# Ten of sixteen experts sorted by token count on the chip, the last four taken in one pass of four column tiles

## The chip, the cores and the metric

The kernel runs on one core of a Trainium2 chip. The metric is device time in microseconds (us); the median of three runs of the kernel before is 483.41 us (481.74 to 483.44). Traces come from the hardware profiler, one execution each. PE is TensorE's matmul, PEld its weight load, DVE is VectorE, ACT is ScalarE, POOL is GpSimd, SP is the engine whose queue issues nearly all DMAs.

## The reference, cut to what matters

A decoder block on 256 tokens (16 meta tokens in front make 272) with 1024 features: two mixers in parallel on a normalised input, then a mixture of 16 experts, then a norm. All of it is float32. The change concerns the experts alone.

```python
def hier_moe(u, wg_r, bg_r, we_r, be_r, w_gate, w_up, w_down):
    t = u.reshape(b * L, d)
    p_group = softmax(t @ wg_r + bg_r)             # 4 groups
    g_val, g_idx = top_k(p_group, 1)
    e_logits = (t @ we_r + be_r).reshape(-1, 4, 4)
    sel = take_along_axis(e_logits, g_idx[:, :, None], axis=1)[:, 0]
    top_v, top_i = top_k(sel, 2)                   # 2 of the group's 4 experts
    top_w = softmax(top_v)
    combine = ...                                  # (tokens, 16): 0 but for two experts
    for e in range(16):                            # w_gate[e], w_up[e]: 1024 x 512; w_down[e]: 512 x 1024
        h = silu(t @ w_gate[e]) * (t @ w_up[e])
        out = out + combine[:, e:e + 1] * (h @ w_down[e])
```

Each of the 256 tokens goes to two experts of one group, so an expert has 32 tokens in the mean. With the reference's inputs (seed 0) the experts 0 to 15 have 37, 31, 32, 36, 25, 24, 24, 27, 50, 39, 35, 38, 26, 32, 27 and 29 tokens; this was worked out from the reference and stands in no trace.

## The kernel before, in words

The program is written in order by hand, engine by engine; nothing reorders it. Up to about 235 us the trace shows the mixers: products with `w_in` and `w_out` in two float32r parts, the SSD and the short convolution between them. From 235 to 252 us stands the router: scores, for each expert the slot of each of its tokens (`ranks`, tile `rk`), and the largest token count (`most`, then the integer `mosti`, which every engine loads into a register).

The weights come as a stream of tiles of 1 MB (128 partitions x 8 KB), issued on SP's queue into a ring of slots in SBUF: `RING` slots that the whole program uses, `RING2` more for the experts. An expert matrix is 2 MB; a tile is a quarter of the rows of a matrix, of both experts of a pair (4 KB of each per partition). There are 96 tiles of experts, 12 to a pair: gate, up, down. When PE is done with a tile, `used(1)` gives its slot to the next tile of the stream; SP waits at that DMA until the slot is free, and everything behind it in SP's program waits too.

The experts go in 8 pairs (loop over `pair`, L1099). An expert has `CAP` = 64 slots; a pair fills the 128 columns of the array. Within a pair:

- `pick` makes a selection matrix P (tokens x 128 slots), `gather3` multiplies the normalised tokens by it and gives X, the tokens of both experts, transposed. The tokens stand in three bf16 parts (`hparts`), made by ACT and DVE in turn during the first pair.
- `half_product` (L965) multiplies X by the weights: for each of 8 slices k of the features, one matmul for each expert, 64 columns of the array each (`tile_position`), 512 wide; each shows as two records in the trace. Gate, then silu on ACT; up, then a product on DVE (`hb`).
- `back` and `turned` give the transposed selection, the weights of the tokens, and hb transposed; the down product is four slices of twice 512.
- `weighed` and `scatter` add the weighted rows to their tokens in four PSUM banks, within the next pair's gate product.

The first product of X for pair 0 is a plain float32 gather in the router; DVE scales it (`rows`, L1003). `weights` on DVE works out the combine weights and their three bf16 parts (`cparts`). After the last pair's up product stands `tc.If(rv > CAP)`: where an expert has more than 64 tokens, `over()` takes all pairs again from further slots; in the traced run it is not taken. The last pair's down product is in three pieces of 512, 256 and 256 columns, and the end of its stream in pieces too; then comes the last norm.

Of the kernel before, what the change touches and what calls it, by code (L numbers as in the profile page):

```python
# [20 lines left out]
RING, RING2 = 21, 3  # L21
# [14 lines left out]
def body(ctx, tc, x, meta_tokens, norm_mix, w_in, ssd_conv_w, ssd_conv_b, dt_bias, A_log, D_skip,  # L36
# [31 lines left out]
    between = []  # L68

    def load(n, pool=None):  # L70
        # the next n tiles of the stream
        for j in range(nload[0], min(nload[0] + n, NW + 96)):
# [28 lines left out]
            stream[j] = w  # L101

# [5 lines left out]
    rk = cp.tile([128, 2, NE], F32, name="rk")  # L108
    comb = cp.tile([128, 2, NE], F32, name="comb")
# [20 lines left out]
    # the meta tokens: partition 8 t + k has features 128 k to 128 k + 127 of token t  # L130
# [26 lines left out]
    # what is small goes between the large ones  # L157
# [29 lines left out]
    # the columns of one product are fewer than the array's  # L187
    f0 = slot("f0").bitcast(F32R)
    G.iota(sl, pattern=[[1, CAP]], base=-1024, channel_multiplier=0, allow_small_or_imprecise_dtypes=True)
# [54 lines left out]
    def x_part(b, n, c0=0, c1=512):  # L244
        # the residual goes to where the product with w_out will be added up
# [27 lines left out]
    def split_hi(i):  # L273
# [67 lines left out]
    def dt_softplus(n):  # L341
        # softplus(a) = max(a, 0) + log(1 + e), e = exp(-|a|); log(1 + e) = 2 atanh(e / (2 + e))
# [18 lines left out]
    def dt_sums():  # L361
        # sums of dA within tokens 0-127 and within tokens 128-271: for the keys ...
# [7 lines left out]
        # ... and for the queries  # L370
# [160 lines left out]
    def sums(key, t, n, kind):  # L531
# [7 lines left out]
        # in two parts that sum to it: one in the even rows, one in the odd ones  # L539
# [99 lines left out]
    # tiles of the ring that are not of the stream: the steps in which they are held  # L639
# [23 lines left out]
    def fill(i):  # L663
        # after step i: as many tiles of the stream as leave room for the others
# [110 lines left out]
    def logits(b, q):  # L775
        # the products of four parts of the features side by side
# [16 lines left out]
    def places(b, step):  # L793
        # how many of a set of four come before each (equal ones: the lower index first)
# [9 lines left out]
        else:  # L804
            # of the first two of their group, whose group is the first: 1 is more than no group
# [3 lines left out]
    def ranks(b):  # L809
        # slot of each token at each of its experts, less 1024; not negative where it isn't one of them  # L810
# [4 lines left out]
        V.scalar_tensor_tensor(rk[:, b], mem[:, b], -1024.0, p, op0=OP.mult, op1=OP.add)  # L815

    def pick(P, pair, b):
        V.tensor_tensor(P[:, b], sl[:, None].to_broadcast([128, 2, CAP]),
                        rk[:, b, 2 * pair:2 * pair + 2][:, :, None].to_broadcast([128, 2, CAP]), op=OP.is_equal)

    def gather(b, q, p, i0=0, i1=4):
        # one mark per bank: the first product in it clears the bank's marks of what has been written
        for i in range(i0, i1):
            T.matmul(p[:, i], hh[:, b].rearrange("p (m k) -> p k m", k=KT)[:, 4 * q + i],
                     P[:, b].rearrange("p s c -> p (s c)"), start=(b == 0 and i == 0), stop=(b == 1),
# [173 lines left out]
    def w_of(pair, kind, q):  # L999
        return stream[NW + 12 * pair + 4 * kind + q]  # L1000
# [234 lines left out]
```

## Time and profile before

| | us |
|---|---|
| median of 3 runs (lowest, highest) | 483.41 (481.74, 483.44) |
| the profiled execution: span from the first to the last instruction | 480.2 |
| PE busy in it | 456.1 |
| DVE, ACT, POOL busy | 234.7, 161.6, 64.8 |
| first product of pair 0, of pair 1, of pair 7 starts at | 252.19, 278.16, 441.98 |
| last down product ends at about | 470.5 |

Of the profiled execution only the span is given; the median of the runs is 3.2 us longer, which is what lies around the span. A busy PE is not PE at its peak: matmuls are pipelined and their ends are modelled, so a time between two starts of a repeated piece says more than a sum of busy times. A wait is read from the bracket behind a row of the timeline: how long the engine stood idle, and what ended it.

### The profile page before, as it was taken

How to read it: one execution, taken by the hardware profiler on the slowest of the kernel's cores; microseconds unless marked ns; L12 is line 12 of the kernel's file. 1: busy time of each engine (PE TensorE's matmuls, PEld its weight loads, DVE VectorE, ACT ScalarE, POOL GpSimd, SP SyncE). 2: the span in 40 equal slices, each digit the busy share in tenths (PEclk: the TensorE clock that was granted, in tenths of full speed). 3: DMA queues.
4: the chain of work that ended last, by engine and by line, in shares of the span. 5: the costliest groups of instructions: out<-in, count | busy, mean ns of one | idle time of the engine just before them, and what ended most of it. 6: DMA issues, size and time to landing. Idle time of an engine off the chain costs nothing. (4 is left out here: it accounts for less than half of the span.)

```text
span 480.2 us, 7357 instructions
## 1 busy us (share of the span) xinstructions
PE 456.1 (95%) x2983; PEld 307.9 (64%) x2983; DVE 234.7 (49%) x467; ACT 161.6 (34%) x256; POOL 64.8 (13%) x36
## 2 busy tenths in 40 slices
PE   6999999899889999999999999999999999999984
PEld 4899899798878999778883535344353535334342
DVE  5779798878895586675446312102021212102223
ACT  5674456455744444544444210101001010100203
POOL 1233234232364141000000000000000000000000
PEclk9999999999998999999999999999999999999998
DMA  6889974255894545996767999999999999999002
GB/s 195 252 271 349 349 275 141 88 176 176 289 412 176 186 166 177 360 363 240 264 261 263 414 407 409 409 410 409 407 410 409 410 408 409 408 408 389 14 3 87
DMA packets 61419, 139.84 MB, mean 291 GB/s; under 512 B 6326, under 2 KB 33350, under 8 KB 61126
## 3 DMA queue, kind: packets, MB, share of 16 engines
q1 hardware_dynamic: 61094, 138.94, 78.5%
q8 instruction: 25, 0.41, 0.3%
q10 hardware_dynamic: 288, 0.39, 0.2%
q14 instruction: 12, 0.10, 0.1%
HBM read 138.26 MB, written 1.06 MB: 290 GB/s over the span
## 5 line engine op out<-in xcount | busy, mean ns | idle before, releaser
L967 PE MATMUL gu<-w,X 128*64 128x512 f32 x512 | 114.8, 595 | 0.0
L967 PEld LDWEIGHTS gu<-w,X 128*64 128x64 f32 x512 | 35.3, 137 | 68.8 <-issue 67.0
L288 ACT ACTIVATE f<-w 128x1024 fp32r<-128x1024 f32 x64 | 67.3, 1054 | 35.6 <-PE acc L320 14.8
L299 POOL TENSOR_TENSOR f<-w,f 128x1024 fp32r<-128x1024 f32 x24 | 59.9, 2495 | 117.9 <-ACT f L288 106.6
L967 PE MATMUL yd<-w,hd 128*64 128x512 f32 (+1 forms) x272 | 56.7, 570 | 0.5 <-DVE hd L977 0.5
L299 DVE TENSOR_TENSOR f<-w,f 128x1024 fp32r<-128x1024 f32 x40 | 48.8, 1219 | 13.9 <-ACT f L288 13.8
L320 PE MATMUL acc<-f,h 128*128 128x512 f32 x192 | 45.4, 393 | 0.0
L1129 DVE TENSOR_TENSOR hb<-hb,gu 128x512 f32<-128x512 f32 x8 | 5.5, 689 | 76.1 <-PE gu L967 71.3
L983 DVE SCALAR_TENSOR_TENSOR Yl<-yd,ws,Yh 128x512 fp32r<-128x512 f32 x14 | 10.5, 751 | 62.3 <-PE yd L967 44.8
L320 PEld LDWEIGHTS acc<-f,h 128*128 128x128 f32 x192 | 35.5, 188 | 8.0 <-issue 0.4
L967 PEld LDWEIGHTS yd<-w,hd 128*64 128x64 f32 x272 | 18.8, 137 | 32.3 <-issue 29.4
L982 ACT ACTIVATE Yh<-yd,ws 128x512 fp32r<-128x512 f32 x14 | 9.6, 688 | 85.4 <-PE yd L967 66.0
L1036 PE MATMUL xp<-P,hh 128*128 128x128 bf16 x224 | 22.1, 225 | 0.0
L1036 PEld LDWEIGHTS <-hh 128*128 128x128 bf16 x224 | 21.1, 147 | 1.1 <-issue 1.1
L1036 PE MATMUL xp<-P,h 128*128 128x128 bf16 x112 | 19.8, 228 | 1.1 <-ACT hb L1113 1.1
L312 PE MATMUL p_b<-uh,f 128*128 128x256 f32 x128 | 17.6, 292 | 2.5 <-DVE h L579 2.0
L961 ACT ACTIVATE PT<-ptp 128x256 fp32r<-128x256 f32 x8 | 3.1, 385 | 49.1 <-PE ptp L957 49.1
L1113 ACT ACTIVATE hb<-gu 128x512 f32<-128x512 f32 x8 | 4.8, 595 | 42.9 <-PE gu L967 42.9
L312 PEld LDWEIGHTS p_b<-uh,f 128*128 128x128 f32 x128 | 16.2, 195 | 3.7 <-issue 2.9
L1003 DVE TENSOR_TENSOR X<-xp,gf 128x512 f32<-128x512 f32 x16 | 11.1, 692 | 15.1 <-PE xp L1036 12.1
L312 PE MATMUL p_xs<-uh,f 128*128 128x272 f32 x128 | 18.0, 293 | 0.0
L312 PE MATMUL p_c<-uh,f 128*128 128x258 f32 x128 | 16.9, 285 | 0.8 <-DVE h L579 0.8
(317 smaller groups left out, 678.8 us busy)
## 6 DMA issues: line engine op xcount, KB each, us to landing
w<-in_expert_w_gate SPq DMA_DIRECT2D x32, 1024.0 KB, 13.9
w<-in_expert_w_up SPq DMA_DIRECT2D x32, 1024.0 KB, 15.1
w<-in_expert_w_down SPq DMA_DIRECT2D x30, 1024.0 KB, 15.2
w<-in_w_in SPq DMA_DIRECT2D x23, 1024.0 KB, 7.9
w<-in_w_out SPq DMA_DIRECT2D x8, 1024.0 KB, 8.1
abc<-adr SPq DMA_DIRECT2D x2, 1024.0 KB, 5.9
w<-in_expert_w_down SPq DMA_DIRECT2D x3, 512.0 KB, 16.6
xt<-in_x SPq DMA_DIRECT2D x4, 256.0 KB, 3.4
```

The costliest lines, as they stand in the source:

```text
L288: A.activation(h, src, AF.Copy)
L299: (G if on_pool(name, c) else V).tensor_tensor(l, src, h.bitcast(F32), op=OP.subtract)
L312: T.matmul(p, st_[:, k, :], mv[:, k, t0:], start=(k == 0 and st_ is terms[0][0] and mv is uh), stop=(k == KT - 1 and mv is ul))
L320: T.matmul(acc[b][n], st_[:, 128 * b:128 * (b + 1)], mv[:, 512 * n:512 * (n + 1)], start=False, stop=False, skip_group_check=True)
L961: A.activation(PT, p[:, 0:256], AF.Copy)
L967: T.matmul(o[64 * s:64 * s + 64], X[:, 128 * k + 64 * s:128 * k + 64 * s + 64], w[:, s, c], start=first_, stop=last_, tile_position=(0, 64 ...
L982: A.activation(Yh, y, AF.Copy, scale=ws)
L983: V.scalar_tensor_tensor(Yl, y, ws, Yh.bitcast(F32), op0=OP.mult, op1=OP.subtract)
L1003: V.tensor_tensor(X[:, 4 * q:4 * q + 4], p, gf[:, 4 * q:4 * q + 4][:, :, None].to_broadcast([128, 4, 128]), op=OP.mult)
L1036: T.matmul(p[:, i], hparts[j][b].rearrange("p (m k) -> p k m", k=KT)[:, 4 * q + i], P[:, b].rearrange("p s c -> p (s c)"), start=(j == b = ...
L1113: A.activation(hb, g, AF.Silu)
L1129: V.tensor_mul(hb, hb, g)
```

## The change

- The experts go in seven units, `UNITS` = 2, 2, 2, 2, 2, 2, 4. The first six experts (`FIXED`) stay at their places. The ten others are sorted by token count on the chip, the most first, so that the last unit has the four with the fewest; there an expert has 32 slots and 32 columns of the array.
- `sort_experts`, on DVE, replaces the two instructions that made `most` and `mosti`. It makes the order of the ten as integers (`order`), sorts their columns of `rk` into 10 further columns (`in_order`), and sets `mosti`. One of the last four with more than 32 tokens counts as over 64, so `over()` would run.
- SP loads `order` into registers; tiles of sorted experts are loaded from an address that is worked out from a register. `weights` sorts the ten columns of `comb` too.
- A tile of the stream is half of one expert's matrix, 8 KB in a row per partition, in place of a quarter of two. Slots are given back as many at a time as the unit has experts, after every second slice pair (`k % 4 == 3`), down after `k % 2`.
- `side_by_side` replaces `half_product`: two or four column tiles, each with its own expert's weights.
- `RING` is 22 in place of 21 (`dynamic_dma_scratch_size=64` goes with it). The end of the stream is in pieces for all four experts, issued in turn.

```diff
-RING, RING2 = 21, 3
+RING, RING2 = 22, 3
+UNITS = 6 * [2] + [4]
+FIXED = 6
+NX = NE + NE - FIXED
...
-                pair, r = divmod(j - NW, 12)
-                kind, q = divmod(r, 4)
+                place, kind, half_ = experts_at[j - NW]
                 src = (expert_w_gate, expert_w_up, expert_w_down)[kind]
-                w = w.rearrange("p (s c) -> p s c", s=2)
-                for c, n in ENDS if j == NW + 95 else HALVES if j == NW + 94 else [(0, 1024)]:
-                    nc.sync.dma_start(w[:, :, c:c + n], raw(src, 2 * pair * D * 512 + 1024 * q + c,
-                                                            [[4096, 128], [D * 512, 2], [1, n]]))
+                if place < FIXED:
+                    rows_ = raw(src, place * D * 512, [[4096, 128], [1, 4096]])
+                else:
+                    rows_ = src[0, bass.ds(chosen[place - FIXED], 1)].rearrange("e a b -> (e a b)").rearrange(
+                        "(p m) -> p m", p=128)
+                if j < NW + 92:
+                    nc.sync.dma_start(w, rows_[:, 2048 * half_:2048 * half_ + 2048])
+                else:
+                    pieces = [(0, 1024)] + [(1024 + c, n) for c, n in ENDS]
+                    rest_.append([(w[:, c:c + n], rows_[:, 2048 + c:2048 + c + n]) for c, n in pieces])
+                    nc.sync.dma_start(*rest_[-1][0])
+                    if j == NW + 95:
+                        for i in range(1, len(pieces)):
+                            for r in rest_:
+                                nc.sync.dma_start(*r[i])
...
+    def in_order(out_, of, t):
+        m = NE - FIXED
+        t = t.rearrange("p (b i j) -> p b i j", b=2, i=m)
+        V.tensor_tensor(t, chain[:, None].to_broadcast([128, 2, m, m]),
+                        of[:, :, None, :].to_broadcast([128, 2, m, m]), op=OP.mult)
+        V.tensor_reduce(out_, t, axis=AX.X, op=OP.add)
+
+    def sort_experts(counts):
+        m, key = NE - FIXED, place
+        t = small("srt", 2 * m * m)
+        c = counts[:, FIXED:NE]
+        V.scalar_tensor_tensor(key, c, float(NE), count16[:, FIXED:NE], op0=OP.mult, op1=OP.subtract)
+        V.tensor_tensor(chain, key[:, None, :].to_broadcast([128, m, m]), key[:, :, None].to_broadcast([128, m, m]),
+                        op=OP.is_gt)
+        V.tensor_reduce(place, chain, axis=AX.X, op=OP.add)
...
+        V.tensor_copy(order, t[:, m * m:m * m + m])
+        in_order(rk[:, :, NE:NX], rk[:, :, FIXED:NE], t)
...
+        V.tensor_tensor(mosti, most, t[:, 0:1], op=OP.max)
...
-    V.tensor_reduce(most, rp[0:1, 96:112], axis=AX.X, op=OP.max)
-    V.tensor_copy(mosti, most)
+    sort_experts(rp[:, 96:112])
...
+        in_order(comb[:, :, NE:NX], comb[:, :, FIXED:NE], sorting)
...
-    def half_product(o, X, w, k, c, first_, last_):
-        for s in range(2):
-            T.matmul(o[64 * s:64 * s + 64], X[:, 128 * k + 64 * s:128 * k + 64 * s + 64], w[:, s, c],
-                     start=first_, stop=last_, tile_position=(0, 64 * s))
+    def side_by_side(o, X, w, k, first_, last_):
+        c = 128 // len(w)
+        for s, ws_ in enumerate(w):
+            T.matmul(o[c * s:c * s + c], X[:, 128 * k + c * s:128 * k + c * s + c], ws_,
+                     start=first_, stop=last_, tile_position=(0, c * s))
...
+    chosen += nc.values_load_multi_w_load_instructions(
+        order[0:1], engines=[mybir.EngineType.SP], min_val=FIXED, max_val=NE - 1,
...
-    for pair in range(8):
-        last = pair == 7
+    for u, ne in enumerate(UNITS):
+        last = u == len(UNITS) - 1
...
-                half_product(g, Xf, w_of(pair, kind, k // 2), k, slice(k % 2 * 512, k % 2 * 512 + 512), k == 0,
-                             k == KT - 1)
-                if k % 2:
-                    used(1)
+                side_by_side(g, Xf, w_of(u, kind, k, 0, 512), k, k == 0, k == KT - 1)
+                if k % 4 == 3:
+                    used(ne)
```

The order of the instructions, at the three places that matter. First DVE at the end of the router, in the kernel before (P is the selection matrix of pair 0, rp the PSUM bank with the counts, xp the gathered tokens):

```order
L818 TENSOR_TENSOR P<-sl,rk 128x128
L904 TENSOR_REDUCE most<-rp 1x1
L905 CAST mosti<-most 1x1
L1003 TENSOR_TENSOR X<-xp,gf 128x512 x2
L925 TENSOR_REDUCE tm<-lg 128x10
```

The same place in the changed kernel, 5 of the sort's 15 instructions left out:

```order
L851 TENSOR_TENSOR P<-sl,rk 128x128
L866 SCALAR_TENSOR_TENSOR place<-rp,count_78 128x10
L867 TENSOR_TENSOR chain<-place 128x100
L869 TENSOR_REDUCE place<-chain 128x10
L871 TENSOR_TENSOR chain<-place,count_78 128x100
L873 TENSOR_TENSOR srt<-chain,count_78 128x100
L875 TENSOR_REDUCE srt<-srt 128x10
L876 CAST order<-srt 128x10
L858 TENSOR_TENSOR srt<-chain,rk 128x200
L860 TENSOR_REDUCE rk<-srt 128x2x10
...
L884 TENSOR_TENSOR mosti<-most,srt 128x1
L1076 TENSOR_TENSOR X<-xp,gf 128x512 x2
```

Fifteen instructions, and not two, stand ahead of the two that scale X for the first product of pair 0.

Then SP's queue at the same time, before:

```order
L99 DMA w_2526<-in_expert_w_down 128x2x1024
L99 DMA w_2528<-in_expert_w_down 128x2x1024
L1095 TENSOR_LOAD mosti
L1095 ISA x2
L99 DMA w_2694<-in_expert_w_down 128x2x1024
L99 DMA w_2700<-in_expert_w_gate 128x2x1024
L99 DMA w_2706<-in_expert_w_gate 128x2x1024
```

And in the changed kernel, with the first loads of sorted experts behind the dots (w is a tile of the stream; ISA is the arithmetic on registers):

```order
L112 DMA w_2533<-in_expert_w_down 128x2048
L112 DMA w_2535<-in_expert_w_down 128x2048
L1170 TENSOR_LOAD mosti
L1170 ISA x2
L1171 TENSOR_LOAD order
L112 DMA w_2743<-in_expert_w_gate 128x2048
L112 DMA w_2745<-in_expert_w_gate 128x2048
...
L112 ISA
L112 DMA w_2908<-in_expert_w_gate 128x2048
L112 ISA
L112 DMA w_2910<-in_expert_w_gate 128x2048
```

All 24 tiles of the first two pairs are now issued ahead of the load of `mosti` (23 before), one more load of registers follows, and each load of a sorted expert has an instruction of its own ahead of it.

Last PE at the start of the last unit, before (acc are the four sums of the output, Yh and Yl the weighted rows of the pair before):

```order
L967 MATMUL yd<-w_3527,hd 64x512 x4
L967 MATMUL gu<-w_3541,X 64x512 x4
L988 MATMUL acc_68<-Yh,PT 128x512
L988 MATMUL acc_68<-Yl,PT 128x512
L988 MATMUL acc_70<-Yh,PT 128x512
L988 MATMUL acc_70<-Yl,PT 128x512
L967 MATMUL gu<-w_3551,X 64x512 x4
```

In the changed kernel:

```order
L1036 MATMUL yd<-w_3392,hd 64x512
L1036 MATMUL gu<-w_3415,X 32x512
L1036 MATMUL gu<-w_3417,X 32x512
L1036 MATMUL gu<-w_3431,X 32x512
L1036 MATMUL gu<-w_3433,X 32x512
L1036 MATMUL gu<-w_3415,X 32x512
L1036 MATMUL gu<-w_3417,X 32x512
L1036 MATMUL gu<-w_3431,X 32x512
L1036 MATMUL gu<-w_3433,X 32x512
L1057 MATMUL acc_68<-Yh,PT 128x512
L1057 MATMUL acc_68<-Yl,PT 128x512
```

For each slice there are now four matmuls of 32 columns, each from a tile of its own, where there were two of 64 columns from one tile.

## Rows read from the trace of the kernel before

**Rows 1.** The page's first part: PE's busy time, share, instructions.

```profile
PE 456.1 (95%) x2983; PEld 307.9 (64%) x2983; DVE 234.7 (49%) x467; ACT 161.6 (34%) x256; POOL 64.8 (13%) x36
```

**Rows 2.** Timeline of PE: start us, us, engine, line, instruction [idle before].

```profile
252.19 13.95 PE L967 MATMUL gu<-w,X 128*64 128x512 f32 x64
267.66 0.22 PE L1036 MATMUL xp<-P,h 128*128 128x128 bf16 x1 [1.13 <-ACT hb L1113]
...
278.16 1.89 PE L967 MATMUL gu<-w,X 128*64 128x512 f32 x8
...
441.98 1.89 PE L967 MATMUL gu<-w,X 128*64 128x512 f32 x8
...
463.42 7.11 PE L967 MATMUL yd<-w,hd 128*64 128x512 f32 x48 [0.51 <-DVE hd L977]
470.45 0.73 PE L988 MATMUL acc<-Yh,PT 128*128 128x512 f32 x2
```

**Rows 3.** Busy time of each engine in stretches of the expert stage.

```profile
core 0: us, PE busy (x) PEld busy (x) DVE busy (x) ACT busy (x) POOL busy (x), PEclk, DMA share, GB/s
268.00:288.00 20.00, 20.00 (x125) 9.13 (x123) 4.28 (x9) 1.59 (x3) 0.00 (x0) 1.00 1.03 409
...
442.00:446.00 4.00, 4.00 (x20) 1.57 (x18) 1.25 (x2) 0.71 (x2) 0.00 (x0) 1.00 0.62 220
```

**Rows 4.** Waits: engine, line, waited for, us in total, times, longest us.

```profile
PEld gu L967 <- DMA w<-in_expert_w_up: 0.6, 2, 0.4
...
PE yp L509 <- DVE h L489: 3.1, 3, 1.3
```

**Rows 5.** Timeline of SP's queue: start us, us from first to last issue.

```profile
254.17 0.38 SPq L99 DMA_DIRECT2D w<-in_expert_w_down  x1
...
368.45 10.10 SPq L99 DMA_DIRECT2D w<-in_expert_w_gate  x4
```

**Rows 6.** Timeline of DVE from the router to the first pair.

```profile
244.59 0.24 DVE L803 TENSOR_REDUCE cnt<-gt 128x20 f32<-128x80 f32 x1
...
248.30 0.16 DVE L904 TENSOR_REDUCE most<-rp 1x1 f32<-1x16 f32 x1 [1.15 <-PE rp L901]
248.50 0.14 DVE L905 CAST mosti<-most 1x1 int32<-1x1 f32 x1
250.40 0.69 DVE L1003 TENSOR_TENSOR X<-xp,gf 128x512 f32<-128x512 f32 x1 [1.76 <-PE xp L824]
...
252.91 0.18 DVE L925 TENSOR_REDUCE tm<-lg 128x10 f32<-128x40 f32 x1
...
256.82 1.22 DVE L1025 TENSOR_TENSOR hh<-hh,h 128x1024 f32<-128x1024 f32 x1
```

**Rows 7.** Timeline of ACT: silu of the first pair.

```profile
267.03 0.58 ACT L1113 ACTIVATE hb<-gu 128x512 f32<-128x512 f32 x1
```

**Rows 8.** Line L1095: engine, instruction, ns min/median/max, first and last start.

```profile
L1095 PEldq TENSOR_LOAD <-mosti x1: 488/488/488, 248.7 to 248.7; - x1
L1095 SPq FUSED_REGOPS  x1: 191/191/191, 249.2 to 249.2; - x1
```

**Rows 9.** Timeline of PE: four tiles of 32 columns, and whole arrays, 128 wide.

```profile
239.53 0.64 PE L780 MATMUL lp<-r,wr 128*32 128x128 f32 x16
...
453.20 1.16 PE L995 MATMUL fp<-fin,o 128*128 128x128 f32 x8
```

**Rows 10.** Timeline of PE and stretches of 1 us after its longest late wait.

```profile
144.37 2.88 PE L312 MATMUL p_b<-uh,f 128*128 128x256 f32 x16 [1.96 <-DVE h L579]
...
145.00:146.00 1.00, 1.00 (x9) 1.00 (x8) 0.00 (x0) 1.00 (x3) 0.27 (x2) 0.71 1.04 414
146.00:147.00 1.00, 1.00 (x6) 1.00 (x6) 0.00 (x0) 0.98 (x2) 1.00 (x1) 0.50 0.56 221
...
148.00:149.00 1.00, 1.00 (x9) 0.78 (x12) 0.01 (x1) 0.24 (x1) 0.14 (x1) 0.58 0.01 4
```

**Rows 11.** Line L99, the loads of experts: us from issue to landing.

```profile
DMA to landing us min/median/max: 5.1/14.7/19.2
```

More of the change, by code (lines that the diff above doesn't have):

```diff
@@ L67, in body @@
     nload = [0, 0]
-    between = []
+    between, rest_, chosen = [], [], []
+    experts_at = []
+    for u, n in enumerate(UNITS):
+        for kind in range(3):
+            for h in range(2):
+                experts_at += [(sum(UNITS[:u]) + i, kind, h) for i in range(n)]
+    tile_at = {e: NW + i for i, e in enumerate(experts_at)}
     def load(n, pool=None):
@@ L107, in body @@
     gf = cp.tile([128, KT], F32, name="gf")
-    rk = cp.tile([128, 2, NE], F32, name="rk")
-    comb = cp.tile([128, 2, NE], F32, name="comb")
+    rk = cp.tile([128, 2, NX], F32, name="rk")
+    comb = cp.tile([128, 2, NX], F32, name="comb")
+    count16 = cp.tile([128, NE], F32, name="count16")
+    chain = cp.tile([128, NE - FIXED, NE - FIXED], F32, name="chain")
+    place = cp.tile([128, NE - FIXED], F32, name="place")
+    order = cp.tile([128, NE - FIXED], I32, name="order")
     fcol = cp.tile([128, KT], F32, name="fcol")
@@ L814, in ranks, with places_of @@
             T.matmul(p, onesb, mem[:, 0], start=False, stop=True)
[L815 to L819, printed above, removed]
+        V.scalar_tensor_tensor(rk[:, b, 0:NE], mem[:, b], -1024.0, p, op0=OP.mult, op1=OP.add)
+    def places_of(u):
+        e = sum(UNITS[:u])
+        e += NE - FIXED if e >= FIXED else 0
+        return slice(e, e + UNITS[u])
@@ L883, in body @@
     busy(1)
-    P = bp.tile([128, 2, 2, CAP], F32, name="P")
+    P = bp.tile([128, 2, 128], F32, name="P")
     pick(P, 0, 0)
@@ L900, in body @@
     for b in range(2):
-        T.matmul(rp[0:1, 96:112], onesb[:, 0:1], mem[:, b], start=(b == 0), stop=(b == 1))
-    most = cp.tile([1, 1], F32, name="most")
-    mosti = cp.tile([1, 1], I32, name="mosti")
-    V.tensor_reduce(most, rp[0:1, 96:112], axis=AX.X, op=OP.max)
-    V.tensor_copy(mosti, most)
+        T.matmul(rp[:, 96:112], onesb, mem[:, b], start=(b == 0), stop=(b == 1))
+    most = cp.tile([128, 1], F32, name="most")
+    mosti = cp.tile([128, 1], I32, name="mosti")
+    sort_experts(rp[:, 96:112])
     for q in range(2):
@@ L944, in weights @@
                 V.tensor_tensor(comb, comb, cparts[:, :, :, i], op=OP.subtract)
-    cparts = wk.tile([128, 2, NE, 3], BF, name="cparts")
+    cparts = wk.tile([128, 2, NX, 3], BF, name="cparts")
+    sorting = wk.tile([128, 2 * (NE - FIXED) ** 2], F32, name="sorting", tag="Yl")
     idb = idt.bitcast(BF).rearrange("p (c h) -> p c h", h=2)[:, :, 1]
@@ L952, in back @@
         p = bank("m", "ptp")
+        n, c = cm.shape[2], 128 // cm.shape[2]
         for b in range(2):
[L954 to L955 removed]
+            T.matmul(p[:, 128 * b:128 * (b + 1)], P[:, b], idb, start=True, stop=True)
+        for s in range(n):
             for b in range(2):
[L957 to L958 removed]
+                T.matmul(p[c * s:c * s + c, 256:259], P[:, b, c * s:c * s + c], cm[:, b, s], start=(b == 0),
+                         stop=(b == 1), tile_position=(0, c * s))
         PT = wk.tile([128, S], F32R, name="PT", tag="PT")
@@ L997, in fin_part, with w_of @@
                       p.rearrange("p (k m) -> p k m", k=4))
-    def w_of(pair, kind, q):
-        return stream[NW + 12 * pair + 4 * kind + q]
+    def w_of(u, kind, k, c, n):
+        per, width = (2, 1024) if kind == 2 else (4, 512)
+        at_ = k % per * width + c
+        e = sum(UNITS[:u])
+        return [stream[tile_at[e + i, kind, k // per]][:, at_:at_ + n] for i in range(UNITS[u])]
     def rows(X, p, q):
@@ L1079, in over @@
                     for k in range(KT):
-                        half_product(g, Xo.rearrange("p k t -> p (k t)"), w[4 * kind + k // 2], k,
-                                     slice(k % 2 * 512, k % 2 * 512 + 512), k == 0, k == KT - 1)
+                        side_by_side(g, Xo.rearrange("p k t -> p (k t)"),
+                                     [w[4 * kind + k // 2][:, e, k % 2 * 512:k % 2 * 512 + 512] for e in range(2)],
+                                     k, k == 0, k == KT - 1)
                     if kind == 0:
@@ L1089, in over @@
                     for k in range(4):
-                        half_product(y, hdo, w[8 + k], k, slice(512 * n, 512 * n + 512), k == 0, k == 3)
+                        side_by_side(y, hdo, [w[8 + k][:, e, 512 * n:512 * n + 512] for e in range(2)], k, k == 0,
+                                     k == 3)
                     weighed(y, wso, Yo)
@@ L1093, in over @@
                         scatter(b, n, PTo, Yo)
-    rv = nc.values_load(mosti, min_val=0, max_val=S)
+    rv = nc.values_load(mosti[0:1], min_val=0, max_val=2 * S)
+    chosen += nc.values_load_multi_w_load_instructions(
+        order[0:1], engines=[mybir.EngineType.SP], min_val=FIXED, max_val=NE - 1,
+        skip_runtime_bounds_check_because="a sum of one of the numbers FIXED to NE - 1 and of zeros")[1]
     left = {}
@@ L1124, in body @@
                 if not last:
-                    Pn = wk.tile([128, 2, 2, CAP], BF, name="P", bufs=2)
+                    Pn = wk.tile([128, 2, 128], BF, name="P", bufs=2)
                     for b in range(2):
-                        pick(Pn, pair + 1, b)
+                        pick(Pn, u + 1, b)
             else:
@@ L1135, in body @@
             hd = turned(hb)
-        PT, ws = back(P, cparts[:, :, 2 * pair:2 * pair + 2])
+        PT, ws = back(P, cparts[:, :, places_of(u)])
         if not last:
```

39 lines of the change are left out of this document (25 added, 14 removed).

## The prediction

> **What bounds the kernel now.** I read the page first: PE is busy for 456.1 of 480.2 us [rows 1]. That alone says little, so the second view was the timeline of PE, between two starts of the same piece. Pair 1 starts at 278.16 and pair 7 at 441.98 [rows 2]; six pairs in 163.82 us are 27.30 us for a pair. The third view was the stretches: in the same time the loads run at 409 GB/s without a pause [rows 3]. A pair has 12 tiles of 1.0486 MB, so at that rate its loads take 12 x 2.564 = 30.8 us, which is more than PE's 27.30. PE can outrun the stream only because it started with two pairs' tiles in the ring. The fourth view was the waits: no engine lost more than 0.6 us to a load of experts [rows 4]. So PE sets the end, by a narrow margin: the last load ends about 2.5 us into the stretch from 442 to 446 (0.62 of 4 us [rows 3]), near 444.5, and the last down product starts at 463.42 [rows 2]. Whatever shortens PE's work by more than some 25 us will meet the stream. That is what the reader is to keep in mind.
>
> **The change part by part.** The sum is made on the profiled span of 480.2 us; the median of the runs is 3.2 us above it, and that is added at the end.
>
> *One unit less.* Eight units become seven: -27.30 us, if the last unit takes as long as a pair. Products of X, gather, transposes, weighing and scattering are as many in the unit of four as in a pair. Only the products with the weights differ.
>
> *The pass of four.* A pair's gate and up products take 13.95 us in 64 records, two tiles of 64 columns at a time [rows 2]: 32 passes of 436 ns. The unit of four has the same 32 passes, each of four records of 32 columns, and 24 passes in its down product (4 slices, 3 pieces, 2 records each). If the tiles run side by side like the two, a pass costs what its width costs, and a little for each further record. The nearest rows: the router's 16 records of 32 columns, 128 wide, in fours side by side, take 0.64 us, so 160 ns for four; whole-array products of the same width and type take 1.16 us for 8, so 145 ns for one [rows 9]. Three further tiles cost 15 ns, 5 ns each. Two more for each of 56 passes are 0.56 us; I take +0.6. Below, the bound is 0; above, it is that two tiles run beside each other and four don't: 13.95 + 7.11 = 21.1 us [rows 2]. I stay near the lower end because rows 9 are that very shape of tile, on this chip, only narrower.
>
> [...]
>
> *The sort on DVE.* It stands ahead of the scaling of X. Durations go with the width: 0.24 us for 80 elements, 0.69 for 512 [rows 6], so 1.04 ns an element; the two narrow ones, 0.16 and 0.14, start 0.20 apart. Eight narrow ones at 0.20, five of 100 elements at 0.26 + 0.04, two of 200 at 0.365 + 0.04 make 1.6 + 1.5 + 0.8 = 3.9 us. Before, DVE was idle for 1.76 us ahead of the first scaling at 250.40; that is the cover. The sort starts at 248.30, as `most` did, and ends at 252.2. X's first half is ready at 252.9, and the first gate product starts then and not at 252.19: +0.75. PE's own load of `mosti` (0.488 us [rows 8]), queued ahead of that product, is done at 252.7, within the same wait. The other half of X is done at 253.5, and the next DVE work, at 252.91 before, is 0.55 late; sorting the weights adds two instructions of 200 elements (0.8), the wider `cparts` 0.1. So the chain of DVE and ACT that makes the bf16 parts, which began at 256.82 [rows 6] and had no slack, is 1.45 us late. At its end on ACT stands the first pair's silu (267.03 [rows 7]), whose bank the gather waits for: PE already lost 1.13 us there [rows 2]. The gather starts at 269.1, not 267.66. PE's delay from all this is +1.45, the earlier 0.75 being part of it. Bounds: 0.5 if the small instructions overlap, 2.5 if each takes 0.3.
>
> *The clock.* That wait of PE grows to 1.13 + 1.45 - 0.75 = 1.8 us. [...]
>
> *SP's queue.* One more load of registers (0.5 us, as PE's) and one register instruction (0.19 [rows 8]) for each sorted load. SP has until PE frees the first two tiles, after half the gate product: 252.9 + 3.5 = 256.4. Later SP issues four loads in 10.1 us [rows 5], 2.5 us each, held only by the rate of the loads themselves; 0.19 us hides in that. Cost 0. Above: the rival on loads below.
>
> *The stream.* Its 24 first tiles are in before pair 0; 72 remain, and the first two go at 256.4. Before, 73 remained and the first went at 254.17 [rows 5]. So at the same rate the stream ends 2.2 us later less one tile of 2.56: near 444.1, as before. Runs of 8 KB in place of 4 KB can only help. In the first unit two tiles come free at a time; the eight of gate and up, free by 267.4, keep the loads busy for 20.5 us from about 257.4, to 278, and the first two of down come free near 276. No hole.
>
> *Who is late then.* The unit of four starts at 441.98 - 27.30 + 1.45 + 0.7 = 416.8; its down product 21.44 us later (463.42 - 441.98), at 438.3, and its last slice at 443.6. The stream's last pieces land at 444.1. So the stream is hidden but for some half a microsecond, and with the longer runs entirely. Cost 0; up to 4 us if the stream has holes.
>
> *The ring's one more slot* matters before 250 us only if PE waits for loads there; its longest wait is for DVE [rows 4], and none of its waits names a DMA. Cost 0, bounds -1 and +1: a load of `w_in` now goes ahead of `adr`.
>
> *The tail* after the last down product, with its wait for the branch, is the same: the last slice sets it, as before.
>
> Sum: -27.30 + 0.6 + 1.45 + 0.7 = -24.55. Span 455.65, time 458.9 us.
>
> **The rivals.**
> 1. *The stream ends last.* For it: 444.1 against 443.6. Holes of b us, or slower service, move the end by b: 444.1 + b + 0.5 for the last piece + 9.75 for the tail (480.2 - 470.45) + 3.2 = 457.6 + b. From b = 1.3 this exceeds the forecast; a hole for every unit's late tiles, 1 us each, gives 464. Against: after 300 us tiles come free faster than they load.
> 2. *Four tiles don't run side by side at full width.* Two by two, it is 458.9 + 20.5 = 479.4, 0.8% faster than before. If the wide pass keeps the whole factor of 1.10 of [rows 9], it costs 2.1 us in place of 0.6: 460.4; a third of the full loss gives 465.3. Against more than that: rows 9. [...]
> 3. *Loads from a register address are served one after the other, and the kernel is slower.* Nothing like it runs in the trace before. A load that has the queue for itself lands 5.1 us after its issue (the least of [rows 11]). Places 6 to 15 have 60 tiles, and the first of them would go 12 x 2.56 us after 257.4, at 288.1. At 5.1 us each the last lands at 594: 594 + 0.5 + 9.75 + 3.2 = 608 us. It decides from the point where the last piece lands at 469.9, PE's old end: (469.9 - 288.1) / 60 = 3.03 us a load, against 2.56 now. Against it: they go on the same queue, in the same shape, and differ by one register instruction.
> 4. *The change doesn't do what it says*: one of the last four experts has over 32 tokens and `over()` runs. Eight turns of 12 tiles are at least 246 us, over 700 in all. With the reference's inputs the four have 24, 26, 27 and 27, so this is all but excluded.
>
> **How the numbers follow.** The forecast has 0.74; by its own bounds (sort 0.5 to 2.5, clock 0 to 1.7, pass 0 to 2, slot 1 either way) it lies between 456 and 462. The stream last: 0.10, 459 to 464. Tiles in part: 0.07, 460 to 466; two by two 0.03. Slow loads 0.05, `over()` 0.01. The range is 455 to 465. A measurement of this kernel tells a difference of about 0.5% (2.4 us) from none. Faster by more than that: the forecast, the stream and the tiles in part, most of two by two, 0.92; the same 0.03; slower 0.05.
>
> **What would show it.** In the profile of the changed kernel: the first gate product near 252.9 and the gather near 269.1 with a wait of some 1.8 us on ACT's silu; pairs 27.3 us apart; in the unit of four, 128 gate and up records in about 14.3 us; loads at 409 GB/s or a little over until near 438 to 444; the tail 9.75 us. Wrong would be a wait of PE on loads over 1 us in the last unit, passes of four well over 450 ns, or a rate that falls where the sorted experts begin.

## The result, and the profile after

The changed kernel takes 462.67 us (median of 4 runs, 462.24 to 463.57), the kernel before 482.64 in the runs beside it (481.74 to 483.44): a ratio of 0.9584, with a 95% interval of 0.9559 to 0.961. It is 4.2% faster. The forecast of 458.9 lies 3.8 us too low. The measured time is inside the stated range of 455 to 465, but outside the 456 to 462 given for the forecast itself; the upper part of the range stood there for the late stream and the slower passes of four, and neither came. That the range holds is in part luck.

In the profiled execution the span went from 480.2 to 461.8 us (its time is 463.57). One unit less is worth -27.3; 8.9 us came back. The timeline of PE in the last unit says where most of it went (start, length, instruction; in brackets the idle time before it and what ended it):

```profile
417.89 1.92 PE L1036 MATMUL gu<-w,X 128*32 128x512 f32 x16
433.17 3.64 PE L1036 MATMUL gu<-w,X 128*32 128x512 f32 x32
440.66 1.10 PE L1043 MATMUL hbp<-idt,hb 128*128 128x128 f32 x4 [3.85 <-PEq L1208]
442.55 9.49 PE L1036 MATMUL yd<-w,hd 128*32 128x512 f32 x96 [0.40 <-DVE hd L1046]
452.07 0.74 PE L1057 MATMUL acc<-Yh,PT 128*128 128x512 f32 x2
```

The same stretch of the kernel before, beside the rows of its start in [rows 2]:

```profile
457.25 3.65 PE L967 MATMUL gu<-w,X 128*64 128x512 f32 x16
461.91 0.72 PE L974 MATMUL hbp<-idt,hb 128*128 128x128 f32 x4 [1.01 <-DVEq L1131]
```

From the end of the last up product (436.81 and 460.90) to the first scatter it takes 15.26 us, and took 9.55: +5.7. Two things make nearly all of it. PE stood idle for 3.85 us in place of 1.01 ahead of the last transposes, waiting for its own sequencer (PEq) at L1208, the branch past the code for experts of over 64 tokens. And then the down product took 9.49 us in place of 7.11, since the granted clock had fallen (0.58 and 0.57 from 440 to 448); the transposes between the two lost the other 0.4 us. The stretches of the changed kernel show both, with the loads (length, busy times of PE, PEld, DVE, ACT and POOL, granted clock, DMA share, GB/s):

```profile
268.00:288.00 20.00, 18.34 (x122) 8.88 (x120) 5.19 (x12) 4.14 (x6) 0.00 (x0) 1.00 1.01 419
436.00:440.00 4.00, 0.81 (x8) 0.00 (x0) 0.69 (x1) 0.00 (x0) 0.00 (x0) 1.00 0.97 343
440.00:444.00 4.00, 2.93 (x22) 1.57 (x26) 0.85 (x2) 0.38 (x1) 0.00 (x0) 0.58 0.55 170
444.00:448.00 4.00, 4.00 (x38) 1.43 (x34) 0.00 (x0) 0.00 (x0) 0.00 (x0) 0.57 0.02 4
448.00:452.00 4.00, 4.00 (x60) 1.56 (x52) 0.00 (x0) 0.67 (x2) 0.00 (x0) 1.00 0.00 0
```

The loads run at 419 GB/s where they ran at 409 [rows 3], and end near 442.2 (0.55 of the stretch from 440). So they are under way while PE's sequencer is in the branch; in the kernel before they had ended at 444.5, nearly 13 us ahead of it. PE waits for them as little as before [rows 4] (us in total, times, longest):

```profile
PEld gu L1036 <- DMA w<-in_expert_w_up: 0.7, 2, 0.4
PEld yd L1036 <- DMA w<-in_expert_w_gate: 0.3, 1, 0.3
```

The branch itself, in the kernel before and in the changed one (nanoseconds, start in us):

```profile
L1131 PEldq COMPARE_BRANCH  x1: 3582/3582/3582, 457.3 to 457.3; - x1
```

```profile
L1208 PEldq COMPARE_BRANCH  x1: 6197/6197/6197, 434.1 to 434.1; - x1
```

The head, where the sort stands. First DVE's sort, 15 instructions between these two, then X's scaling; then PE at the second router gather, the first gate product and the gather for the next unit:

```profile
250.43 0.17 DVE L866 SCALAR_TENSOR_TENSOR place<-rp,count 128x10 f32<-128x10 f32 x1 [1.06 <-PE rp L966]
...
253.81 0.16 DVE L884 TENSOR_TENSOR mosti<-most,srt 128x1 int32<-128x1 f32 x1
253.88 1.28 DVE L1076 TENSOR_TENSOR X<-xp,gf 128x512 f32<-128x512 f32 x2
```

```profile
250.25 4.05 PE L889 MATMUL xp<-P,hh 128*128 128x128 f32 x16
254.71 13.96 PE L1036 MATMUL gu<-w,X 128*64 128x512 f32 x64 [0.41 <-DVE X L1076]
270.71 0.22 PE L1109 MATMUL xp<-P,h 128*128 128x128 bf16 x1 [1.66 <-ACT hb L1190]
```

Before, the same gather started at 248.19:

```profile
248.19 4.07 PE L824 MATMUL xp<-P,hh 128*128 128x128 f32 x16
```

So 2.06 us were lost ahead of the sort, in code that the change hardly touches. What stands out there is the granted clock: it fell to 0.50 three times, and once in the kernel before (from 145.4 to 148.8, [rows 10]). Stretches of 4 us around the three:

```profile
10.00:14.00 4.00, 3.72 (x11) 2.44 (x12) 3.26 (x9) 2.88 (x8) 0.00 (x0) 0.57 0.50 115
92.00:96.00 4.00, 4.00 (x26) 3.44 (x25) 2.45 (x11) 0.00 (x0) 0.00 (x0) 0.57 0.33 113
146.00:150.00 4.00, 3.71 (x20) 3.74 (x21) 0.48 (x2) 3.75 (x5) 3.27 (x2) 0.63 0.66 264
```

From the gather's start to the next unit's it is 20.46 us, and was 19.47 (267.66 - 248.19 [rows 2]): the sort costs 0.99. The account is thus -27.3 + 2.06 + 0.99 + 5.7 = -18.55, against -18.4 measured. That the falls of the clock make the 2.06 us is a reading of these rows; no run was made to show it.

### The profile page after: what moved, and what is told of

It is laid out like the page before. It is cut to its first block, busy times and chain, and to the rows that moved or that the text cites. A ratio compares the mean times of both kernels' runs of the same rounds, so it can differ in the third digit from the quotient of the medians.

```text
span 461.8 us, 7412 instructions
## 1 busy us (share of the span) xinstructions
PE 435.7 (94%) x2937; PEld 300.1 (65%) x2937; DVE 234.0 (51%) x473; ACT 159.0 (34%) x252; POOL 64.7 (14%) x37
## 5 line engine op out<-in xcount | busy, mean ns | idle before, releaser
L1036 PE MATMUL gu<-w,X 128*64 128x512 f32 (+1 forms) x512 | 100.5, 595 | 0.4 <-DVE X L1076 0.4
L1036 PEld LDWEIGHTS gu<-w,X 128*64 128x64 f32 (+1 forms) x512 | 31.2, 130 | 60.2 <-issue 58.2
L325 DVE TENSOR_TENSOR f<-w,f 128x1024 fp32r<-128x1024 f32 x40 | 48.7, 1218 | 14.0 <-ACT f L314 13.8
L1036 PE MATMUL yd<-w,hd 128*64 128x512 f32 (+2 forms) x288 | 52.0, 585 | 0.4 <-DVE hd L1046 0.4
L1036 PEld LDWEIGHTS yd<-w,hd 128*64 128x64 f32 (+1 forms) x288 | 16.6, 135 | 30.5 <-issue 27.7
L1052 DVE SCALAR_TENSOR_TENSOR Yl<-yd,ws,Yh 128x512 fp32r<-128x512 f32 x12 | 9.0, 751 | 53.6 <-PE yd L1036 38.5
L1109 PEld LDWEIGHTS <-hh 128*128 128x128 bf16 x192 | 18.1, 147 | 1.6 <-issue 1.6
L1109 PE MATMUL xp<-P,hh 128*128 128x128 bf16 x192 | 19.0, 225 | 0.0
L1109 PE MATMUL xp<-P,h 128*128 128x128 bf16 x96 | 17.0, 227 | 1.7 <-ACT hb L1190 1.7
L338 PE MATMUL p_z<-uh,f 128*128 128x256 f32 x128 | 17.9, 295 | 0.0
L338 PE MATMUL p_h<-uh,f 128*128 128x258 f32 x128 | 17.1, 287 | 0.0
```

Of the source, the lines that this page charges most:

```text
L325: (G if on_pool(name, c) else V).tensor_tensor(l, src, h.bitcast(F32), op=OP.subtract)
L338: T.matmul(p, st_[:, k, :], mv[:, k, t0:], start=(k == 0 and st_ is terms[0][0] and mv is uh), stop=(k == KT - 1 and mv is ul))
L1036: T.matmul(o[c * s:c * s + c], X[:, 128 * k + c * s:128 * k + c * s + c], ws_, start=first_, stop=last_, tile_position=(0, c * s))
L1052: V.scalar_tensor_tensor(Yl, y, ws, Yh.bitcast(F32), op0=OP.mult, op1=OP.subtract)
L1109: T.matmul(p[:, i], hparts[j][b].rearrange("p (m k) -> p k m", k=KT)[:, 4 * q + i], P[:, b], start=(j == b == 0), stop=(j == 2 and b == 1))
```

## The experiments

Theory A: the branch costs those 5.7 us, and it does by how far it leaps while the stream fills the DMA queues. Rivals: the unit of four itself (its column tiles, its loads), addresses from registers, or chance. Each has four to ten executions, beside nine to thirteen of the kernel before, whose medians were 482.19 to 483.14. "Distance" below is that from the end of the last up product to the first scatter (before 9.55, after 15.26).

**The kernel after once more** (no edit).

> The changed kernel once more, on one chip with the next three. In its first profile three pieces lie off the forecast: the second router gather starts at 250.25 us and not 248.19, PE waits 3.85 us at the branch before the last transposes (1.01 before), and the clock then falls to 0.5 for 6.8 us, so the last down product takes 9.5 us in place of 7.1. If the branch and the clock belong to the program, they are here again and the time is 462.7 us within 1. If the 2.06 us before 250 us are an accident of the clock in the mixers (one fall of 3.4 us at 92.7 us that the kernel before did not show), the gather's start may lie anywhere from 248.2 to 250.3.

462.38 us (461.97 to 462.73), ratio 0.9577 (0.9539 to 0.9615). The branch takes 6137 ns, the distance is 14.9. But the gather starts at 249.28, with one fall of the clock ahead of it. So the late loss repeats, and the early one in part only.

**No branch.**

```diff
-            with tc.If(rv > CAP):
-                over()
```

> The changed kernel without the conditional overflow pass (its branch and its body are left out; the reference's inputs never take it). Theory A, the branch costs PE the wait: the wait falls to about 0.9 us, which is DVE's product hb, the clock stays at 1.0, the last down product takes 7.1 us; 2.9 + 2.4 + 0.4 = 5.7 us less, 457.0 us. Rival B, the wait is the chain of hb and the transposes themselves, late through the pass of four: the wait stays near 3.9 us, and 462.7 us.

455.59 us (455.42 to 458.66), ratio 0.9457 (0.9408 to 0.9507). The distance is 9.53:

```profile
435.25 0.75 PE L1043 MATMUL hbp<-idt,hb 128*128 128x128 f32 x4 [0.88 <-DVE hb L1206]
436.78 7.09 PE L1036 MATMUL yd<-w,hd 128*32 128x512 f32 x96 [0.52 <-DVE hd L1046]
443.90 0.73 PE L1057 MATMUL acc<-Yh,PT 128*128 128x512 f32 x2
```

The branch is the whole late loss. This profile has no fall of the clock at all ahead of the tail, and its gather starts at 247.81, with the sort in place: the early loss does not belong to the changed code. The time is 1.4 us under the forecast of 457.0 because the early loss is absent too.

**The branch with the stream done** (the last eight tiles are not loaded, the last down product takes the gate's).

```diff
-            if nload[0] < NW + 96:
+            if nload[0] < NW + 88:
...
+        from_ = 0 if u == len(UNITS) - 1 and kind == 2 else kind
...
```

> The changed kernel with the last eight tiles of the stream not loaded (the last unit's down product reads its gate tiles instead, so the output is not the reference's); the branch stays. The stream then ends about 20 us earlier, near 422 us, and no load runs while PE takes the branch. Theory A1, the branch is long because PE's next instructions come by DMA beside the stream: the branch takes 3.6 us in place of 6.2, PE waits about 1.0 us, the clock stays at 1.0, 457.0 us. Rival A2, the branch is longer in this program whatever the DMA queues do: 6.2 us, a wait of 3.9, 462.7 us.

458.64 us (455.95 to 460.28). The branch takes 3617 ns, PE idles 1.20, the down product takes 7.09, the distance is 9.7. The time is 1.6 us over the forecast of 457.0: the profile has three early falls (gather at 250.79). With no load under way, the branch and what follows it came as forecast.

```profile
L1210 PEldq COMPARE_BRANCH  x1: 3617/3617/3617, 434.6 to 434.6; - x1
```

```profile
438.56 0.72 PE L1043 MATMUL hbp<-idt,hb 128*128 128x128 f32 x4 [1.20 <-PEq L1210]
440.06 7.09 PE L1036 MATMUL yd<-w,hd 128*32 128x512 f32 x96 [0.52 <-DVE hd L1046]
```

**The kernel before with seven idle loads past its branch.**

```diff
+                    for j in range(7):
+                        h = free[j]
+                        wd = slot("dummy%d" % j, h).rearrange("p (s c) -> p s c", s=2)
+                        nc.sync.dma_start(wd, raw(expert_w_gate, 2 * j * D * 512,
+                                                  [[4096, 128], [D * 512, 2], [1, 1024]]))
```

> The kernel before with seven more loads of 1 MB, that nothing reads, issued behind the end of its stream, so that loads run until about 462 us, past the branch at 457.3 us. Theory A1 (DMA traffic makes the branch long): the branch takes about 6.2 us in place of 3.6, PE waits 3.6 to 3.9 us in place of 1.0, the clock falls, the last down product takes 9.5 us: 482.6 + 5.3 = 487.9 us. Rival A2 (the branch belongs to the program): 482.6 us within 1.

486.31 us (485.55 to 488.62), ratio 1.0077 (1.0046 to 1.0109): the loss appears in the kernel before too.

```profile
L1136 PEldq COMPARE_BRANCH  x1: 6218/6218/6218, 457.2 to 457.2; - x1
```

```profile
463.71 0.72 PE L974 MATMUL hbp<-idt,hb 128*128 128x128 f32 x4 [2.90 <-PEq L1136]
465.21 8.80 PE L967 MATMUL yd<-w,hd 128*64 128x512 f32 x48 [0.51 <-DVE hd L977]
```

It is smaller than the forecast 487.9: PE waits 2.90 us and not 3.6 to 3.9, and the distance is 13.1. PE's sequencer comes to the branch 3.6 us ahead of the end of the last up product here, as in the pairs below, and 2.7 us ahead of it in every run where it stands there in the unit of four, which has twice as many records in the same time (32 in 3.64 us, 16 in 3.65). So about 0.9 us of the longer wait in the kernel after comes with the unit of four, and the rest with the stream.

**The branch with a short leap.**

```diff
-                over()
+                T.transpose(bank('m', 'hbp')[:, 0:128], hb[:, 0:128], idt)
```

> The kernel after with the code behind the branch cut down to one transpose; the branch itself stays where it was, and is not taken either way with these inputs, so the output is the same. Theory D (the branch is dear because what follows it lies far away in the program, past the code that it leaps, and must be fetched from memory while the stream fills the queues): with a target close by the branch takes under 1.5 us, TensorE idles about 1 us before the last transposes, the clock stays up and the time is 456 to 458. Rival D1 (any branch on the register takes its 6 us beside the stream, wherever it goes, since the sequencer fetches anew): the branch takes 6 us, and the time stays at 462 to 463.

458.4 us (457.85 to 459.46), ratio 0.9498 (0.9465 to 0.9531). At the same place, beside the same stream, the branch takes 228 ns, and the distance is 9.53. The time is a little above the forecast 456 to 458; the profile has two early falls (gather at 250.42). Past one transpose it costs 0.23 us, past all of `over()` 6.20.

```profile
L1208 PEldq COMPARE_BRANCH  x1: 228/228/228, 434.3 to 434.3; - x1
```

**A third of the code behind the branch.**

```diff
-            for r in range(1, S // CAP):
+            for r in range(1, 2):
```

> The kernel after with a third of the code behind the branch (one round of the loop over further 64 tokens instead of three, which these inputs do not reach); the branch stays where it was. Theory D2 (what counts is whether the target lies in the part of the program that has been fetched already; with a leap over some 130 of TensorE's listed instructions instead of 390 it still does not): the branch takes 6 us as in the kernel after, 461 to 463. Rival D3 (the time grows with the length of the leap): the branch takes 2 to 4 us and the time is 458 to 460.

460.18 us (458.46 to 464.86), ratio 0.9561 (0.951 to 0.9611). Both theories were off. The branch takes 357 ns, the distance is 12.5: a wait of 1.50 us follows a few instructions later with no releaser in the profile, and the clock falls after it (0.79 and 0.78 from 436 to 444):

```profile
436.35 0.21 PE L1024 MATMUL ptp<-cparts,P 128*32 128x3 bf16 x5
438.06 0.21 PE L1024 MATMUL ptp<-cparts,P 128*32 128x3 bf16 x3 [1.50 <-issue]
438.18 8.79 PE L1036 MATMUL yd<-w,hd 128*32 128x512 f32 x96
```

No view names that wait. A target that had been fetched, and a next piece of the program that had not, would fit; that is a reading and was not shown. The traces also hold packets of the kind "instruction", of 16 KB. The pages count them (queue, packets, MB, share), two fewer without the branch and with the short leap (second line) than in the kernel after (first line):

```profile
q8 instruction: 25, 0.41, 0.4%
```

```profile
q8 instruction: 23, 0.38, 0.3%
```

By their times in the traces of the two kernels, the first such packet behind the far branch starts 1.0 us after the branch in the kernel before (458.28), where no load is under way, and 3.6 us after it in the kernel after (437.72), beside the loads. The packet itself takes 1.1 us in both, and the branch ends 1.4 to 1.5 us behind it in both. So the 2.6 us between the two branches lie ahead of that packet. Whose instructions a packet holds is not recorded; that PE's branch waits for this one is a reading of these times.

**No sort** (experts in the order of their index, constant addresses).

```diff
-                if place < FIXED:
+                if True:
...
-    sort_experts(rp[:, 96:112])
+    V.tensor_reduce(most, rp[:, 96:112], axis=AX.X, op=OP.max)
+    V.tensor_copy(mosti, most)
...
```

> The kernel after without the sort: all experts in the order of their index, their addresses constants; the last unit of four is then experts 12 to 15, which have 26, 32, 27 and 29 tokens with these inputs, so that the output is the same. Half-matrix tiles, 22 slots and the unit of four stay. Theory B (the sort costs only the stretch of VectorE before the second gather, and loads with an address from a register cost nothing in the stream): from the second gather to the first gate product 4.0 to 4.2 us instead of 4.5, the rest as in the kernel after, stream at 418 to 421 GB/s: ratio 0.955 to 0.959, some 1 us under the kernel after at most. Rival B1 (addresses from registers are dearer: more instructions on SP, a later start of each load): the stream is faster by 1% or more and TensorE waits less on loads, 3 us or more under the kernel after.

459.95 us (458.23 to 461.33), ratio 0.953 (0.9487 to 0.9572). The first gate product starts 3.98 us after the gather (4.46 with the sort), the next gather waits 1.14 us (1.66), the stream has 417 to 421 GB/s and the branch takes 6117 ns: the sort costs about 1 us and its addresses nothing. The ratio is a little lower than forecast. Between the two profiles (spans of 457.3 and 461.8 us) the other 3.5 us are 2.0 ahead of the sort, where this profile has one fall of the clock and that one three, and 1.4 behind the last up product (distance 13.8), where the lowered clock cost the down product less (8.58 us); the runs don't tell why.

**Pairs, with the new tiles and the 22nd slot, no sort** (to the edit above comes this one).

```diff
-UNITS = 6 * [2] + [4]
+UNITS = 8 * [2]
...
-                if j < NW + 92:
+                if j < NW + 94:
```

> As the run without the sort, and the experts in eight units of two again: of the change only the tiles of half a matrix and the 22nd slot are left. Theory C (the whole gain is the eighth pass: 27.3 us of TensorE, and the tiles alone give nothing): the time of the kernel before within 1.5 us, so 481.5 to 484.5; the stream runs at 418 GB/s against 409 and ends a few us earlier than in the kernel before, while TensorE goes on to the same time. Since the stream ends far ahead of the branch, the branch takes 3.6 us and no clock falls after it. Rival C1 (the tiles' larger runs per partition and the 22nd slot carry part of the gain): 479 or less.

483.46 us (480.9 to 485.55, 10 runs), ratio 1.0013 (0.9986 to 1.004): the time of before. The stream ends near 438.9 in place of 444.5, and nothing comes of it. With the runs above: the whole gain is the unit that is gone.

**The branch behind the last scatter.**

```diff
-            with tc.If(rv > CAP):
-                over()
-            A.activation(s3[:, 0:1], eps, AF.Sqrt)
...
+    with tc.If(rv > CAP):
+        over()
+    A.activation(s3[:, 0:1], eps, AF.Sqrt)
```

> The kernel after, with the branch past the code for experts of more than 64 tokens moved from ahead of the last transposes to behind the last scatter, and the load of the square root's table behind it; nothing is left out. Theory A (the branch costs 5.7 us because it stands ahead of the last unit's transposes, where TensorE's sequencer is 6.1 us in it and the clock then falls): the last gate product to the first scatter is as without a branch, 9.5 us in place of 15.3, TensorE idles under 1.3 us before the last transposes and the last down product takes 7.1 us; behind the scatters the branch now stands on ScalarE's and VectorE's way to the norm. The stream has ended some 10 us before, so it takes about 3.6 us there as in the quiet runs, of which ScalarE can have passed a part while TensorE still scatters: 1 to 4 us are given back, and the time is 459 to 462. Rival A2: all of the branch lies beside the last scatters, because ScalarE and VectorE have nothing to do then, and only the table's load of 1.3 us is added: 457 to 458.5. Rival A3: behind the scatters each engine is late by all of the branch and by its join: 464 or more, no gain.

461.27 us (458.34 to 461.48), ratio 0.9533 (0.949 to 0.9576). The distance is 9.6, but from the first scatter to the end it is 12.8 us (9.73 in the kernel after): ACT's first square waits for PE's branch, which is 3.5 us here.

```profile
451.43 0.60 ACT L1264 ACTIVATE o<-acc 128x512 f32<-128x512 f32 x1 [2.21 <-PEq L1253]
```

**The branch between the last down product and the scatters.**

```diff
-            with tc.If(rv > CAP):
-                over()
...
+    with tc.If(rv > CAP):
+        over()
     for b in range(2):
         scatter(b, 0, PT, [Yh])
```

> The kernel after with the branch between the last down product and the scatters: the weighed products are copied out of the accumulators first, the last unit's two small tiles get places of their own, the square root's table is loaded ahead of the branch as in the kernel after, and again at the end of the code that the branch leaps. Nothing is left out. Theory A (the branch is cheap where the stream has ended and TensorE waits for ScalarE anyway): TensorE's sequencer comes to the branch some 2.6 us before the last down product ends, is 3.5 us in it, as in the quiet runs, and the first scatter comes 0.4 to 1.0 us later than without a branch (9.5 us after the last gate and up product, so 10 to 10.6 against 15.3 in the kernel after); no fall of the clock after 436 us; 456 to 459.5 by the number of falls before 250 us, which vary from run to run. Rival A3 (each engine's leap and the join after it stand on the way to the norm): 460 or more.

458.98 us (458.21 to 459.2), ratio 0.95 (0.9475 to 0.9525). The distance is 11.4, more than forecast: PE's sequencer came to the branch at 443.6, 1.9 us ahead of the product's end and not 2.6. The clock stays at 1.0.

```profile
447.36 0.71 PE L1057 MATMUL acc<-Yh,PT 128*128 128x512 f32 x2 [1.89 <-PEq L1246]
```

**The same, and the code behind the branch as a loop at run time.**

```diff
-            for r in range(1, S // CAP):
+            with tc.For_i(1, S // CAP, 1):
```

> The run with the branch between the last down product and the scatters, and the rounds over further 64 tokens as a loop at run time in place of three copies, so that the code behind the branch is a third as long; nothing is left out. From the run with a third of the code: TensorE's branch then takes 0.4 us in place of 3.6, and a fetch of 1.5 us follows a few instructions later, here beside the scatters and after the stream, so shorter, if at all. Theory A: the first scatter comes 9.5 to 10.2 us after the last gate and up product instead of 11.4, and 1 to 2 us go: 456.5 to 458 with the same number of clock falls before 250 us (two). Rival: the fetch lands inside the scatters and costs what the branch did: 458.5 to 459.5.

458.32 us (455.43 to 459.6), ratio 0.9509 (0.9475 to 0.9543). The branch takes 469 ns, the distance is 9.8 and the tail behind it 9.65:

```profile
443.75 0.70 PE L1057 MATMUL acc<-Yh,PT 128*128 128x512 f32 x2 [0.26 <-PEq L1246]
```

The median lies between the two forecasts and decides nothing; the distance does. The branch's cost is gone but for 0.3 us, and nothing of the computation is left out. This version beats both kernels; against the one above, the medians don't tell them apart, because what happens ahead of 250 us moves them by more than the difference (gather at 249.32 and 247.36 in the two profiles).

## Why the prediction was right or wrong, point by point

- *One unit less.* Right. Units start 27.3 us apart, as pairs did, and the run in pairs shows that nothing else gives anything.
- *The pass of four.* 0 and not +0.6. From the first gate product of the last unit to the end of its up product it is 18.92 us (436.81 - 417.89), and 18.92 in pair 7 (460.90 - 441.98). Sixteen records of 32 columns take 1.92 us. Eight of 64 columns took 1.89 [rows 2]. Rival 2 falls: here four column tiles, 512 wide, cost a pass of two.
- *The sort.* The mechanism was right, at each step: first gate product late, the gather waiting for ACT's silu by 1.66 us (forecast 1.8). The size is 0.99 and not 1.45, mostly because the fifteen instructions take 3.5 us (250.43 to 253.97) in place of 3.9.
- *The clock.* Wrong. No run shows the 0.7 us that the sum has for the clock: after the wait of 1.66 us at the gather it stayed at 1.00 (268 to 288). It fell after the branch (0.58 and 0.57 from 440 to 448), and at three early places. The fall behind the branch, in no term of the sum, cost 2.4.
- *SP's queue, the stream, the ring.* Right: no single wait of PE for a load over 0.4 us, the rate does not fall where sorted experts begin (419 GB/s from 268 to 420, in runs of 8 KB; 409 in runs of 4 KB [rows 3]), and the stream ends near 442 (forecast 438 to 444). The register instruction of a sorted load takes 37 to 51 ns and not 0.19 us. Rivals 1, 3 and 4 fall.
- *The tail.* This is the step that failed: "with its wait for the branch, is the same". The part behind the last down product is the same (9.73 us against 9.75). The branch stands ahead of that product, and was costed at nothing because in the trace of before PE waited 1.01 us there, hardly more than for the product on DVE. But the branch took 3.58 us of PE's sequencer there too, and was covered: it ended at 460.85, the last up product at 460.90. The step read the wait that was left as the whole cost. Beside the loads the branch takes 6.20 us, and with the shorter lead of the unit of four only 2.7 of them are covered; the fall of the clock comes on top. The prediction had worked out that the stream would end near 444 and the last unit start near 417, so that the branch would now stand beside the loads; it asked only which data PE waits for. None of the three signs that it named as wrong appeared, because this step had none.
- *Around the span.* 3.2 us is too much, and is not what lies around the span: in every later run time and span are 1.7 to 2.1 us apart, so the execution profiled before was about 1.4 us under its median.
- *The range.* Added up, the bounds of the four terms behind 456 to 462 reach from 455.7 to 463.4, and slow loads and `over()` make 0.06 and not 0.05. Neither decides. The miss is in a term put at nothing, and the range held because it had been widened for rivals that fell.

In the span the forecast missed by 6.15 us (461.8 - 455.65): 5.7 by the branch and 2.06 ahead of the sort, less 0.46 for the sort, 0.6 for the pass and 0.7 for the clock at the gather; 0.15 stays unexplained.

## What to carry to other kernels

When work is taken out of one engine, list what will now run at the same time as the transfers that did not shrink, branches too: here PE's branch past `over()` took 6.20 us beside the loads, 3.62 with the stream done, and 0.23 past one transpose. Put such a branch behind the last load and where its engine waits anyway, and keep the code that it leaps short. Here that was worth about 4 us out of 463.

## What the runs showed of the hardware that was not expected

- The time of one and the same far branch on PE: 3.4 to 3.6 us with no load of weights under way (before, the stream done, pairs, the two moved branches), 6.1 to 6.2 beside the loads (after, its repetition, no sort, the idle loads; 343 GB/s from 436 to 440 in the kernel after). ACT's and DVE's branches at the same line take 50 and 72 ns. In the kernel after ACT's next instruction starts within 0.7 us; DVE's next waits for PE, so that nothing is seen there.
- The clock did not follow from the length of PE's wait alone. At the start of the program the kernel after waited 1.52 us and ran the next eight products, in 1.77 us, at a lowered clock (0.57 from 10 to 14); its repetition waited 2.34 us and ran them in 1.32, at 1.00:

```profile
10.28 1.77 PE L280 MATMUL up<-idt,un 128*128 128x128 f32 x8 [1.52 <-DVE un L248]
```

```profile
10.42 1.32 PE L280 MATMUL up<-idt,un 128*128 128x128 f32 x8 [2.34 <-DVE un L248]
```

- The number of such falls ahead of 250 us varied from none to three among nine profiles of kernels that are alike up to there, and the second gather's start between 247.4 and 250.8 us, later as a rule with more falls, though not strictly. In the four profiles without the sort it started between 248.1 and 248.5, with one or two falls each; whether that is more than chance is not settled. A difference below 3 us in a single run of this kernel is no evidence. What decides them stays open.
